# State space branch of a hybrid decoder block: constants of the preparation made once for all blocks

## The chip, the cores and the metric

The kernel runs on one core of a Trainium2 chip. The metric is the device time of one execution in microseconds (us). Three executions of the kernel before took 3461.62, 3467.05 and 3470.55 us; the median, 3467.05 us, is the time that the prediction is made against.

## What is computed

A decoder block for 2048 tokens of width 1024: norm, one projection, a state space branch and a sparse attention branch side by side, gates, an output projection, and a SwiGLU network. The change touches the state space branch alone. For each of 32 groups (16 channels in, 64 complex states) the reference computes

```python
abar = exp(A * dt)                                   # complex, per group and state
b    = coef * einsum('gnp,blgp->blgn', B, u)         # complex
s_l  = abar * s_(l-1) + b_l                          # over the 2048 tokens
y    = einsum('gpn,blgn->blgp', C_re, s_r) - einsum('gpn,blgn->blgp', C_im, s_i) + D * u
```

and then a gelu and a gated linear layer.

## The kernel before

**The branch by chunks.** The kernel cuts the 2048 tokens into 256 chunks of 8 (TC = 8, NCH = 256). Two groups lie on the 128 partitions (2 x 64 states) and are called a pair here: there are 16 pairs (NS), worked off in 8 blocks of two (NBLK = 8, SB = 2). For each block `ssm` (line 1340) needs some matrices that depend on the parameters only: G = C times the powers 0 to 8 of abar, E = B times the powers 7 to 0, transposed to ET, M, which carries the outputs within a chunk (it is filled by DMAs from K0, the product of B and G, with D on its diagonal), and pc, the 256 phases by which the chunks' states are turned so that a real scan can run over them.

**Two streams.** `prepare` (line 1353) makes these matrices for one block after another, mostly on POOL: complex products by `cmul` (line 1232), six operations each, a seventh to negate. G and E are made pair by pair (lines 1363 to 1374). Bk, the padded B, is cleared and filled per block (1377 to 1382), K0 is a product on PE copied out by ACT (1383 to 1392), D is added (1394 to 1397), M is cleared (1398, 1399) and filled by 16 DMAs (1402 to 1406), ET comes from PE and ACT (1407 to 1414), and pc from eight doublings, rows of 1, 2, 4 ... 128 phases for two pairs (1416 to 1426). A block is begun when the block two before it is solved (1355).

`solve` (line 1435) takes a block's inputs U, transposes them (Ut), multiplies by ET, turns by pc, scans on DVE, turns back into S (1480 to 1492; POOL clears its first column, 1483 and 1484), has POOL clear F and ACT copy Gr and Gi into it (1495 to 1502), multiplies S by F and Ut by M on PE, and copies the sum out as Y (1503 to 1517). `gelu` (1521) ends the block while the next is solved. All three use one PSUM bank ("sp"), one step after another; F lies in the buffer of `ee`.

**What sets the order.** Each engine works off its own queue in order. A planner (`Pace`, from line 52) lays these queues out when the kernel is built: streams are generators that yield what they wait for, and `Pace` takes the first stream whose need is met at PE's planned time, in the order state space branch, attention, dense part (`run`). Every instruction is booked at an estimated cost; on POOL that is 2.25 ns an element and 0.07 us:

```python
    RATE = {"DVE": (1.05e-3, 0.07), "ACT": (0.84e-3, 0.06), "POOL": (2.25e-3, 0.07)}   # line 58
            cost = size * r + c
```

The profile shows the helper's line, 206, for all of them, so the rows are told apart by their tiles. Beside the state space branch run the first four tiles of attention (scores, top-k search on DVE and ACT, softmax) and, filling PE, the gate matmuls of the dense part: tiles gps of 24 matmuls in two PSUM banks, evicted by ACT to gsg, with weights gw split into two parts by whichever of POOL, DVE and ACT the planner thinks free (`Loader.split`). After the state space branch comes its gated layer (`glu`, line 1557), and only then (`gated`) the rest of attention and the dense blocks, whose matmuls are called f.

Of the kernel before, what the change touches and what calls it, by code (L numbers as in the profile page):

```python
# [12 lines left out]
F32 = mybir.dt.float32  # L13
# [4 lines left out]
AF = mybir.ActivationFunctionType  # L18
ALU = mybir.AluOpType
# [16 lines left out]
G = 32  # L36
NST = 64
PG = 16
SW = G * PG
TC = 8  # L40
# [11 lines left out]
class Pace:  # L52
# [95 lines left out]
    def at(self, eng, *what):  # L148

        return lambda: self.when(eng, what) + (None,)  # L150
# [215 lines left out]
class Block:  # L366
# [851 lines left out]
            tt(s, s, q, op=ALU.mult)  # L1218
        return s, v

    def cmul(self, e, outr, outi, ar, ai, br, bi, t1, t2, neg_i=False):

        e.tensor_tensor(t1, ar, br, op=ALU.mult)
        e.tensor_tensor(t2, ai, bi, op=ALU.mult)
        e.tensor_tensor(outr, t1, t2, op=ALU.subtract)
        e.tensor_tensor(t1, ar, bi, op=ALU.mult)
        e.tensor_tensor(t2, ai, br, op=ALU.mult)
        e.tensor_tensor(outi, t1, t2, op=ALU.add)
        if neg_i:
            e.tensor_tensor(outi, self.zeros[:, :1].to_broadcast(list(outi.shape)), outi, op=ALU.subtract)  # L1230

    def ssm_params(self, pr, wk, ps_t, queue):

        nc, a = self.nc, self.a
        NS = G // 2
# [22 lines left out]
        for n in ("C_re", "C_im"):  # L1258
            t = pr.tile([128, NS, PG], F32, name=n)
            ap = a[n]  # L1260
            for b in range(2):
                raw = wk.tile([128, 2, NST], F32, name=f"{n}{b}")
                for sp in range(8):
                    o = ap.offset + (b * 16 + sp * 2) * PG * NST
                    sync.dma_start(raw[sp * PG:(sp + 1) * PG],
                                      bass.AP(tensor=ap.tensor, offset=o, ap=[[NST, PG], [PG * NST, 2], [1, NST]]))

                def turn(raw=raw, t=t, b=b):
                    ps = ps_t.tile([128, 512], F32, name="tp")
                    nc.tensor.transpose(ps[:, :128], raw.rearrange("p a n -> p (a n)"), self.ident)  # L1270
                    nc.scalar.copy(t[:, b * 8:(b + 1) * 8].rearrange("p s c -> p (s c)"), ps[:, :128])
                turns.append(turn)
            C.append(t)
        ar, ai = A["A_re"], A["A_im"]
# [65 lines left out]
    def ssm(self, st, params):  # L1340
# [8 lines left out]
        NEVER = ("PE", 1e9, None)  # L1349
        made = deque()  # L1350
        taken = [0]

        def prepare():
            for blk in range(NBLK):
                yield lambda: self.pace.idle("POOL") if blk < taken[0] + 2 else NEVER
                s0 = blk * SB
                ss = slice(s0, s0 + SB)

                Gr, Gi = (wk.tile([128, SB, TC + 1, PG], F32, name=f"G{n}", bufs=2) for n in "ri")
                Er, Ei = (wk.tile([128, SB, TC, PG], F32, name=f"E{n}") for n in "ri")  # L1360
                t1 = wk.tile([128, SB, TC + 1, PG], F32, name="t1")
                t2 = wk.tile([128, SB, TC + 1, PG], F32, name="t2")
                for sp in range(SB):
                    q = s0 + sp
                    shp = [128, TC + 1, PG]
                    pa = [z[:, q, :, None].to_broadcast(shp) for z in (ap_r, ap_i)]
                    cc = [z[:, q, None, :].to_broadcast(shp) for z in C]
                    yield self.pace.idle("POOL", ap_i)
                    cmul(gp, Gr[:, sp], Gi[:, sp], cc[0], cc[1], pa[0], pa[1], t1[:, sp], t2[:, sp], neg_i=True)
                    shp = [128, TC, PG]  # L1370
                    pa = [z[:, q, TC - 1::-1, None].to_broadcast(shp) for z in (ap_r, ap_i)]
                    bb = [z[:, q, None, :].to_broadcast(shp) for z in Bb]
                    yield self.pace.idle("POOL")
                    cmul(gp, Er[:, sp], Ei[:, sp], bb[0], bb[1], pa[0], pa[1], t1[:, sp, :TC], t2[:, sp, :TC])

                yield self.pace.idle("POOL")
                Bk = wk.tile([128, 2, SB, 2, PG], F32, name="Bk")
                gp.memset(Bk, 0.0)
                for i in range(2):
                    for g2 in range(2):  # L1380
                        pl = slice(g2 * 64, (g2 + 1) * 64)
                        gp.tensor_copy(Bk[pl, i, :, g2], Bb[i][pl, ss])
                yield at("PE", Bk, Gr, Gi, psp.free_at("sp"))
                ps = psp.tile([128, 512], F32, name="sp")
                for sp in range(SB):
                    o = ps[:32, sp * 128:(sp + 1) * 128]
                    nc.tensor.matmul(o, Bk[:, 0, sp].rearrange("p a c -> p (a c)"),
                                     Gr[:, sp, :TC].rearrange("p t c -> p (t c)"), start=True, stop=False)
                    nc.tensor.matmul(o, Bk[:, 1, sp].rearrange("p a c -> p (a c)"),
                                     Gi[:, sp, :TC].rearrange("p t c -> p (t c)"), start=False, stop=True)  # L1390
                K0 = wk.tile([32, SB, TC, PG], F32, name="K0")
                nc.scalar.copy(K0.rearrange("p s t c -> p (s t c)"), ps[:32, :SB * 128])
                yield self.pace.idle("POOL", K0)
                dd = wk.tile([32, SB, PG], F32, name="dd")
                gp.tensor_tensor(dd, eye[:, None, :].to_broadcast([32, SB, PG]),
                                 Ds[:, ss, None].to_broadcast([32, SB, PG]), op=ALU.mult)
                gp.tensor_tensor(K0[:, :, 0], K0[:, :, 0], dd, op=ALU.add)
                M = wk.tile([128, GB, 128], F32, name="M", bufs=2)
                gp.memset(M, 0.0)
                Mv = M.rearrange("p (s a) c -> p s a c", a=2)  # L1400
                yield at("SP", K0, M)
                for ta in range(TC):
                    for g2 in range(2):
                        nc.sync.dma_start(Mv[ta * PG:(ta + 1) * PG, :, g2, ta * PG:],
                                          K0[g2 * PG:(g2 + 1) * PG].rearrange("p s t c -> p s (t c)")
                                          [:, :, :128 - ta * PG])
                ET = wk.tile([128, 2, SB, 128], F32, name="ET", bufs=2)
                for i, E in enumerate((Er, Ei)):
                    yield at("PE", E, psp.free_at("sp"), wk.free_at("ET", 2) if i == 0 else 0.0)
                    ps = psp.tile([128, 512], F32, name="sp")  # L1410
                    for sp in range(SB):
                        nc.tensor.transpose(ps[:, sp * 128:(sp + 1) * 128],
                                            E[:, sp].rearrange("p t c -> p (t c)"), self.ident)
                    nc.scalar.copy(ET[:, i].rearrange("p s n -> p (s n)"), ps[:, :SB * 128])

                pc = [wk.tile([128, SB, NCH], F32, name=f"pc{n}", bufs=2) for n in "ri"]
                t1, t2 = (wk.tile([128, SB, NCH // 2], F32, name=f"pt{n}", tag=f"t{n}") for n in "12")
                yield self.pace.idle("POOL", wt[1])
                gp.memset(pc[0][:, :, 0:1], 1.0)
                gp.memset(pc[1][:, :, 0:1], 0.0)  # L1420
                for j in range(NW):
                    n = 1 << j
                    wr, wi = (z[:, ss, j:j + 1].to_broadcast([128, SB, n]) for z in wt)
                    cmul(gp, pc[0][:, :, n:2 * n], pc[1][:, :, n:2 * n], pc[0][:, :, :n], pc[1][:, :, :n], wr, wi,
                         t1[:, :, :n], t2[:, :, :n])
                    yield self.pace.idle("POOL")
                made.append((Gr, Gi, M, ET, pc))

        def load(blk):
            U = wk.tile([128, 2, GB, 128], F32, name="U")  # L1430
# [4 lines left out]
        def solve(blk):  # L1435
            s0 = blk * SB
            U = Us.popleft()
            yield lambda: at("PE") if made else NEVER
            Gr, Gi, M, ET, pc = made.popleft()
# [51 lines left out]
            dv.tensor_tensor(x2, sc[1][:, :, c1], pc[0][:, :, c1], op=ALU.mult)  # L1491
            dv.tensor_tensor(Si[:, :, 1:], x1, x2, op=ALU.add)
            yield at("DVE")

            yield at("POOL", wk.free_at("ee"))
            F2 = wk.tile([128, 2, SB, 2, 128], F32, name="F2", tag="ee")
            gp.memset(F2, 0.0)
            yield at("ACT", F2)
            for i, z in enumerate((Gr, Gi)):
                for g2 in range(2):  # L1500
                    pl = slice(g2 * 64, (g2 + 1) * 64)
                    nc.scalar.copy(F2[pl, i, :, g2], z[pl, :, 1:].rearrange("p s t c -> p s (t c)"))
# [483 lines left out]
```

## Time and profile before

| | |
|---|---|
| three executions | 3461.62, 3467.05, 3470.55 us |
| the profiled execution | 3462.75 us |
| its span | 3460.6 us |
| busy: PE, DVE, ACT, POOL | 3201.6, 2133.6, 1261.8, 706.1 us |
| preparation of the eight blocks (first G to last phase) | about 366 to 746 us |
| state space branch, last output written | about 823 us |

The page gives shares of the whole span; the stages have different limits, so the rows below are cut to windows, given in microseconds from the span's start. "PE sp L206 <- ACT F L206: 19.0, 4, 6.3" reads: PE, about to write the tile sp, waited for ACT's writing of F, 19.0 us in total, 4 times, at most 6.3. In a timeline the bracket at a line's end is the idle time before it and what ended it. PEclk is the share of TensorE's full clock that was granted.

### The profile page before, as it was taken

Reading aid. Unit: us, or ns where it says so; the run is one execution under the profiler, and the core shown is the slowest. Engines: PE = TensorE matmul, PEld = TensorE weight load, DVE = VectorE, ACT = ScalarE, POOL = GpSimd, SP = SyncE. Lnnn points to the kernel's source line nnn. Section 1 sums busy time; section 2 is a strip of 40 time slices with the busy share of each in tenths; the row PEclk is TensorE's granted clock in tenths of the full one; section 3 lists DMA queues with packets and bytes.
Section 4 is the critical chain, followed back from the end, with each engine's and each line's share of the span. In section 5 each row is a group of like instructions: output and inputs, shape, how many; then the busy total and the mean of one; then the engine's idle time right before and its main releaser. Section 6 shows DMA issues by size and latency. Waiting matters only on the chain. (4 is left out here: it accounts for less than half of the span.)

```text
span 3460.6 us, 44348 instructions
## 1 busy us (share of the span) xinstructions
PE 3201.6 (93%) x16292; PEld 2698.5 (78%) x16292; DVE 2133.6 (62%) x4306; ACT 1261.8 (36%) x2187; POOL 706.1 (20%) x1003
## 2 busy tenths in 40 slices
PE   6999999898878999989889999988899999999999
PEld 5889777676756888767688888767788888798887
DVE  4565665656496666788776766996856664222222
ACT  3141444445542544465024444771233442010000
POOL 3333686852213122244100000001000000000000
PEclk8999999999988999999999999999999999999999
DMA  4834333433448566567755233556453324755544
GB/s 134 248 119 121 117 110 89 147 124 105 146 148 300 208 212 228 182 232 244 286 184 194 97 133 135 194 195 242 176 200 121 134 86 152 282 214 215 195 170 182
DMA packets 321529, 605.69 MB, mean 175 GB/s; under 512 B 52896, under 2 KB 205216, under 8 KB 290592
## 3 DMA queue, kind: packets, MB, share of 16 engines
q1 hardware_dynamic: 321312, 602.86, 49.9%
q8 instruction: 128, 2.10, 0.3%
q14 instruction: 89, 0.73, 0.1%
HBM read 434.71 MB, written 166.89 MB: 174 GB/s over the span
## 5 line engine op out<-in xcount | busy, mean ns | idle before, releaser
L206 PE MATMUL f<-h,ww 128*128 128x512 f32 (+1 forms) x4416 | 1012.8, 383 | 3.0 <-DVE h L206 1.4
L206 PEld LDWEIGHTS f<-h,ww 128*128 128x128 f32 x4416 | 800.6, 190 | 159.9 <-DVE h L206 2.2
L206 PE MATMUL f<-wd,at 128*128 128x512 f32 x2112 | 530.8, 403 | 60.4 <-ACT at L206 31.9
L206 PEld LDWEIGHTS f<-wd,at 128*128 128x128 f32 x2112 | 403.5, 194 | 156.3 <-ACT at L206 27.9
L206 PE MATMUL gps<-hT,gw 128*128 128x512 f32 x1536 | 390.5, 404 | 17.3 <-ACT gsg L206 14.7
L206 ACT ACTIVATE jka<-S,tr 128x1024 bf16<-128x1024 f32 (+6 forms) x217 | 305.6, 1408 | 172.4 <-DVE tr L206 127.0
L206 PEld LDWEIGHTS gps<-hT,gw 128*128 128x128 f32 x1536 | 287.9, 192 | 81.5 <-ACT gsg L206 17.3
L206 DVE TENSOR_TENSOR x<-f,x 128x512 f32<-128x512 f32 x352 | 237.2, 686 | 91.3 <-PE f L206 90.5
L206 PE MATMUL mm<-w,hT 128*128 128x512 f32 (+1 forms) x1152 | 282.2, 403 | 7.4 <-DVE hT L206 7.1
L206 DVE SCALAR_TENSOR_TENSOR t<-t,f 128x512 f32<-128x512 f32 (+1 forms) x124 | 82.3, 664 | 329.5 <-PE f L206 284.4
L206 PEld LDWEIGHTS mm<-w,hT 128*128 128x128 f32 x1152 | 242.3, 241 | 32.5 <-DVE hT L206 8.5
L206 DVE TENSOR_TENSOR tl<-pt,th 128x512 fp32r<-128x512 f32 (+1 forms) x288 | 183.9, 658 | 131.7 <-ACT th L206 130.4
L206 ACT CAST th<-pt 128x512 fp32r<-128x512 f32 (+1 forms) x288 | 156.0, 563 | 233.5 <-PE pt L206 231.5
L206 POOL TENSOR_TENSOR g<-g,g 128x512 f32<-128x512 f32 x32 | 42.1, 1317 | 915.9 <-issue 551.8
L206 PE MATMUL f<-act,ww 128*128 128x512 f32 x768 | 190.8, 410 | 29.2 <-DMA act<-act 9.0
L206 PE MATMUL f<-ww,mg 128*128 128x256 f32 x1536 | 197.6, 291 | 18.3 <-DMA ww<-wc 10.0
L206 PEld LDWEIGHTS f<-ww,mg 128*128 128x128 f32 x1536 | 193.8, 199 | 21.3 <-issue 8.5
L206 PEld LDWEIGHTS f<-act,ww 128*128 128x128 f32 x768 | 150.8, 199 | 69.0 <-issue 14.3
L206 ACT ACTIVATE P<-P,m 128x1024 f32<-128x1024 f32 (+7 forms) x192 | 172.1, 899 | 72.6 <-DVE m L206 72.0
L206 PE MATMUL lg<-kk,q 128*128 128x512 f32 (+1 forms) x640 | 184.1, 390 | 5.8 <-DMA kk<-kk 3.7
L206 ACT ACTIVATE t<-f 128x512 f32<-128x512 f32 (+1 forms) x92 | 53.0, 576 | 331.7 <-PE f L206 331.6
L206 ACT CAST at<-t 128x512 fp32r<-128x512 f32 (+1 forms) x92 | 55.2, 600 | 325.2 <-DVE t L206 325.1
(347 smaller groups left out, 4577.1 us busy)
## 6 DMA issues: line engine op xcount, KB each, us to landing
ww<-wc SPq DMA_DIRECT2D x180, 1024.0 KB, 5.0
wd<-wc SPq DMA_DIRECT2D x66, 1024.0 KB, 8.5
wc<-ww SPq DMA_DIRECT2D x60, 1024.0 KB, 7.8
raw<-in_w_in_dram SPq DMA_DIRECT2D x104, 256.0 KB, 3.3
wc<-wd SPq DMA_DIRECT2D x22, 1024.0 KB, 7.5
x<-in_x_dram SPq DMA_DIRECT2D x32, 512.0 KB, 5.2
gate<-gsg SPq DMA_DIRECT2D x64, 256.0 KB, 2.2
g<-gate SPq DMA_DIRECT2D x64, 256.0 KB, 5.3
```

The lines of the kernel that those rows point to most:

```text
L206: return f(*args, **kw)
```

## The change

All in the state space branch:

- G and E are made for both pairs of a block in one complex product. The minus of G's imaginary part is taken into C_im when it is transposed (ACT scales by -1), so the negation goes.
- Bk (padded B, now for all 16 pairs, filled by four copies on ACT), dd (D on its diagonal) and the zeros of M and F are made once, ahead of the first block. M and F have two fixed buffers each, taken in turn, whose zeros stay.
- The first 32 phases of all 16 pairs are made once, into p0, in block 0; each block copies its 32 and doubles three times, to 64, 128 and 256.
- F is filled in `prepare`, by the same four copies on ACT per block, right after E has been issued and ahead of K0; the clearing in `solve` is gone. G has one buffer instead of two, and F one of its own.

```diff
-    def cmul(self, e, outr, outi, ar, ai, br, bi, t1, t2, neg_i=False):
+    def cmul(self, e, outr, outi, ar, ai, br, bi, t1, t2):
...
-                    nc.scalar.copy(t[:, b * 8:(b + 1) * 8].rearrange("p s c -> p (s c)"), ps[:, :128])
+                    nc.scalar.activation(t[:, b * 8:(b + 1) * 8].rearrange("p s c -> p (s c)"), ps[:, :128], AF.Copy,
+                                         scale=sign)
...
         def prepare():
+            yield self.pace.idle("POOL")
+            Bk = wk.tile([128, 2, NS, 2, PG], F32, name="Bk")
+            gp.memset(Bk, 0.0)
+            for i in range(2):
+                for g2 in range(2):
+                    pl = slice(g2 * 64, (g2 + 1) * 64)
+                    nc.scalar.copy(Bk[pl, i, :, g2], Bb[i][pl])
+            dd = wk.tile([32, NS, PG], F32, name="dd")
+            gp.tensor_tensor(dd, eye[:, None, :].to_broadcast([32, NS, PG]), Ds[:, :, None].to_broadcast([32, NS, PG]),
+                             op=ALU.mult)
+            Ms = [wk.tile([128, GB, 128], F32, name=f"M{i}") for i in range(2)]
+            Fs = [wk.tile([128, 2, SB, 2, 128], F32, name=f"F{i}") for i in range(2)]
+            for z in Ms + Fs:
+                gp.memset(z, 0.0)
+            p0 = [wk.tile([128, NS, N0], F32, name=f"p0{n}") for n in "ri"]
...
-                    cmul(gp, Gr[:, sp], Gi[:, sp], cc[0], cc[1], pa[0], pa[1], t1[:, sp], t2[:, sp], neg_i=True)
...
-                    cmul(gp, Er[:, sp], Ei[:, sp], bb[0], bb[1], pa[0], pa[1], t1[:, sp, :TC], t2[:, sp, :TC])
...
+                tt(t1, cr, pr, op=ALU.mult)
+                tt(t2, ci, pi, op=ALU.mult)
+                tt(Gr, t1, t2, op=ALU.add)
+                tt(t1, ci, pr, op=ALU.mult)
+                tt(t2, cr, pi, op=ALU.mult)
+                tt(Gi, t1, t2, op=ALU.subtract)
...
+                cmul(gp, Er, Ei, bb[0], bb[1], pa[0], pa[1], t1[:, :, :TC], t2[:, :, :TC])
+                F2 = Fs[blk % 2]
+                yield at("ACT", Gi)
+                for i, z in enumerate((Gr, Gi)):
                     for g2 in range(2):
                         pl = slice(g2 * 64, (g2 + 1) * 64)
-                        gp.tensor_copy(Bk[pl, i, :, g2], Bb[i][pl, ss])
+                        nc.scalar.copy(F2[pl, i, :, g2], z[pl, :, 1:].rearrange("p s t c -> p s (t c)"))
...
-                M = wk.tile([128, GB, 128], F32, name="M", bufs=2)
-                gp.memset(M, 0.0)
+                M = Ms[blk % 2]
...
-                for j in range(NW):
+                for j in range(N0.bit_length() - 1 if blk else 0, NW):
                     n = 1 << j
...
+                    if n == N0:
+                        for z in range(2):
+                            gp.tensor_copy(pc[z][:, :, :N0], p0[z][:, ss])
...
-            yield at("POOL", wk.free_at("ee"))
-            F2 = wk.tile([128, 2, SB, 2, 128], F32, name="F2", tag="ee")
-            gp.memset(F2, 0.0)
-            yield at("ACT", F2)
-            for i, z in enumerate((Gr, Gi)):
-                for g2 in range(2):
-                    pl = slice(g2 * 64, (g2 + 1) * 64)
-                    nc.scalar.copy(F2[pl, i, :, g2], z[pl, :, 1:].rearrange("p s t c -> p s (t c)"))
```

## Rows read from the trace of the kernel before

**Rows 1.** The page, busy time of the engines over the span.
```profile
PE 3201.6 (93%) x16292; PEld 2698.5 (78%) x16292; DVE 2133.6 (62%) x4306; ACT 1261.8 (36%) x2187; POOL 706.1 (20%) x1003
```
**Rows 2.** Busy time by window: length, PE, PEld, DVE, ACT, POOL, PEclk, DMA share, GB/s.
```profile
366.00:746.00 380.00, 342.72 (x1700) 271.39 (x1700) 230.24 (x549) 174.78 (x389) 294.35 (x712) 0.94 0.38 116
...
1011.00:3460.00 2449.00, 2307.51 (x11886) 1951.29 (x11884) 1523.22 (x2834) 830.64 (x1306) 232.54 (x135) 0.97 0.53 194
```
**Rows 3.** Waits of PE, 366 to 825 us: total, times, longest.
```profile
PE sp L206 <- ACT F L206: 19.0, 4, 6.3
PE sp L206 <- POOL pcr L206: 5.8, 1, 5.8
PE sp L206 <- POOL Bk L206: 5.2, 4, 2.8
...
PE sp L206 <- ACT Y L206: 1.8, 2, 1.0
```
**Rows 4.** Timeline, 402 to 496 us: start, duration, engine, operation, tiles, count.
```profile
402.44 3.02 PE L206 MATMUL gps<-hT,gw 128*128 128x512 f32 x12
...
485.91 0.73 DVE L206 TENSOR_TENSOR S<-sct,ee 128x510 f32<-128x510 f32 x1
...
491.78 0.95 POOL L206 MEMSET F<- 128x1024 f32 x1
...
492.77 0.82 ACT L206 COPY F<-Gr 64x256 f32<-64x256 f32 x2 [7.32 <-POOL F L206]
...
493.73 2.05 PE L206 MATMUL sp<-F,S 128*128 128x256 f32 x4 [5.79 <-POOL pcr L206]
```
**Rows 5.** Timeline of PE alone, two other waits.
```profile
421.49 0.64 PE L206 MATMUL sp<-Gr,Bk 128*32 128x128 f32 x2 [2.82 <-POOL Bk L206]
...
733.36 2.05 PE L206 MATMUL sp<-F,S 128*128 128x256 f32 x4 [4.19 <-ACT F L206]
```
**Rows 6.** Busy time by window again; the clock is the third number from the right.
```profile
420.00:745.00 325.00, 292.05 (x1468) 232.22 (x1468) 196.15 (x425) 147.61 (x329) 249.39 (x599) 0.93 0.38 116
490.00:500.00 10.00, 6.27 (x15) 4.95 (x16) 5.73 (x14) 2.69 (x7) 9.06 (x21) 0.66 0.34 94
```
**Rows 7.** Groups of POOL's instructions by form, 366 to 746 us: count, busy us, mean ns.
```profile
L206 POOL TENSOR_TENSOR gw<-raw,gw 128x512 fp32r<-128x512 f32 x13 | 19.8, 1521 | 21.5 <-ACT gw L206 21.3
...
L206 POOL COPY Bk<-Bb 64x32 f32<-64x32 f32 x32 | 9.8, 306 | 1.6
L206 POOL TENSOR_TENSOR t<-C_im,pwi 128x144 f32<-128x144 f32 x16 | 9.0, 560 | 0.0
...
L206 POOL TENSOR_TENSOR Gi<-zeros,Gi 128x144 f32<-128x144 f32 x16 | 6.8, 428 | 1.3
L206 POOL MEMSET F<- 128x1024 f32 x7 | 6.7, 953 | 0.0
L206 POOL TENSOR_TENSOR pcr<-pt,pt 128x256 f32<-128x256 f32 x8 | 6.3, 790 | 0.6
...
L206 POOL TENSOR_TENSOR pcr<-pt,pt 128x128 f32<-128x128 f32 x8 | 3.7, 458 | 0.6
...
L206 POOL TENSOR_TENSOR pcr<-pt,pt 128x2 f32<-128x2 f32 x8 | 3.5, 434 | 0.6
...
L206 POOL TENSOR_TENSOR pcr<-pt,pt 128x64 f32<-128x64 f32 x8 | 2.6, 320 | 0.6
L206 POOL TENSOR_TENSOR pcr<-pt,pt 128x32 f32<-128x32 f32 x8 | 2.1, 260 | 0.6
```
**Rows 8.** ACT, 366 to 825 us: its wait for F, and the copies of Gr into F.
```profile
ACT F L206 <- POOL F L206: 36.0, 6, 10.7
...
L206 ACT COPY F<-Gr 64x256 f32<-64x256 f32 x16 | 6.4, 403 | 36.1 <-POOL F L206 36.0
```
**Rows 9.** Timeline of PE, 836 to 838 us, at the start of the gated layer.
```profile
837.19 1.22 PE L206 MATMUL gps<-hT,gw 128*128 128x512 f32 x2 [9.29 <-ACT gsg L206]
```
**Rows 10.** Timeline of PE, 1671 to 1673 us, in a dense block.
```profile
1671.48 2.08 PE L206 MATMUL f<-wd,at 128*128 128x512 f32 x4 [15.52 <-ACT at L206]
```

More of the change, by code (lines that the diff above doesn't have):

```diff
@@ L1228, in cmul @@
         e.tensor_tensor(outi, t1, t2, op=ALU.add)
-        if neg_i:
-            e.tensor_tensor(outi, self.zeros[:, :1].to_broadcast(list(outi.shape)), outi, op=ALU.subtract)
     def ssm_params(self, pr, wk, ps_t, queue):
@@ L1266, in ssm_params, with turn @@
                                       bass.AP(tensor=ap.tensor, offset=o, ap=[[NST, PG], [PG * NST, 2], [1, NST]]))
-                def turn(raw=raw, t=t, b=b):
+                def turn(raw=raw, t=t, b=b, sign=-1.0 if n == "C_im" else 1.0):
                     ps = ps_t.tile([128, 512], F32, name="tp")
                     nc.tensor.transpose(ps[:, :128], raw.rearrange("p a n -> p (a n)"), self.ident)
-                    nc.scalar.copy(t[:, b * 8:(b + 1) * 8].rearrange("p s c -> p (s c)"), ps[:, :128])
+                    nc.scalar.activation(t[:, b * 8:(b + 1) * 8].rearrange("p s c -> p (s c)"), ps[:, :128], AF.Copy,
+                                         scale=sign)
                 turns.append(turn)
@@ L1351, in ssm @@
         taken = [0]
+        NS, N0 = G // 2, 32
         def prepare():
+            yield self.pace.idle("POOL")
[13 more added lines that the diff above has]
+            p0 = [wk.tile([128, NS, N0], F32, name=f"p0{n}") for n in "ri"]
             for blk in range(NBLK):
@@ L1357, in prepare @@
                 ss = slice(s0, s0 + SB)
-                Gr, Gi = (wk.tile([128, SB, TC + 1, PG], F32, name=f"G{n}", bufs=2) for n in "ri")
+                Gr, Gi = (wk.tile([128, SB, TC + 1, PG], F32, name=f"G{n}") for n in "ri")
                 Er, Ei = (wk.tile([128, SB, TC, PG], F32, name=f"E{n}") for n in "ri")
@@ L1362, in prepare @@
                 t2 = wk.tile([128, SB, TC + 1, PG], F32, name="t2")
[L1363 to L1368, printed above, removed]
-                    cmul(gp, Gr[:, sp], Gi[:, sp], cc[0], cc[1], pa[0], pa[1], t1[:, sp], t2[:, sp], neg_i=True)
[L1370 to L1373, printed above, removed]
-                    cmul(gp, Er[:, sp], Ei[:, sp], bb[0], bb[1], pa[0], pa[1], t1[:, sp, :TC], t2[:, sp, :TC])
+                shp = [128, SB, TC + 1, PG]
@@ new lines, in prepare @@
+                pr, pi = (z[:, ss, :, None].to_broadcast(shp) for z in (ap_r, ap_i))
+                cr, ci = (z[:, ss, None, :].to_broadcast(shp) for z in C)
+                yield self.pace.idle("POOL", ap_i)
+                tt = gp.tensor_tensor
+                tt(t1, cr, pr, op=ALU.mult)
[4 more added lines that the diff above has]
+                tt(Gi, t1, t2, op=ALU.subtract)
@@ L1376, in prepare @@
+                shp = [128, SB, TC, PG]
+                pa = [z[:, ss, TC - 1::-1, None].to_broadcast(shp) for z in (ap_r, ap_i)]
+                bb = [z[:, ss, None, :].to_broadcast(shp) for z in Bb]
                 yield self.pace.idle("POOL")
-                Bk = wk.tile([128, 2, SB, 2, PG], F32, name="Bk")
-                gp.memset(Bk, 0.0)
-                for i in range(2):
+                cmul(gp, Er, Ei, bb[0], bb[1], pa[0], pa[1], t1[:, :, :TC], t2[:, :, :TC])
+                F2 = Fs[blk % 2]
@@ L1386, in prepare @@
                     o = ps[:32, sp * 128:(sp + 1) * 128]
-                    nc.tensor.matmul(o, Bk[:, 0, sp].rearrange("p a c -> p (a c)"),
+                    nc.tensor.matmul(o, Bk[:, 0, s0 + sp].rearrange("p a c -> p (a c)"),
                                      Gr[:, sp, :TC].rearrange("p t c -> p (t c)"), start=True, stop=False)
-                    nc.tensor.matmul(o, Bk[:, 1, sp].rearrange("p a c -> p (a c)"),
+                    nc.tensor.matmul(o, Bk[:, 1, s0 + sp].rearrange("p a c -> p (a c)"),
                                      Gi[:, sp, :TC].rearrange("p t c -> p (t c)"), start=False, stop=True)
@@ L1393, in prepare @@
                 yield self.pace.idle("POOL", K0)
[L1394 to L1397, printed above, removed]
-                M = wk.tile([128, GB, 128], F32, name="M", bufs=2)
-                gp.memset(M, 0.0)
+                gp.tensor_tensor(K0[:, :, 0], K0[:, :, 0], dd[:, ss], op=ALU.add)
+                M = Ms[blk % 2]
                 Mv = M.rearrange("p (s a) c -> p s a c", a=2)
@@ L1418, in prepare @@
                 yield self.pace.idle("POOL", wt[1])
-                gp.memset(pc[0][:, :, 0:1], 1.0)
-                gp.memset(pc[1][:, :, 0:1], 0.0)
-                for j in range(NW):
-                    n = 1 << j
-                    wr, wi = (z[:, ss, j:j + 1].to_broadcast([128, SB, n]) for z in wt)
-                    cmul(gp, pc[0][:, :, n:2 * n], pc[1][:, :, n:2 * n], pc[0][:, :, :n], pc[1][:, :, :n], wr, wi,
-                         t1[:, :, :n], t2[:, :, :n])
+                if blk == 0:
+                    u1, u2 = (t.rearrange("p s c -> p (s c)").rearrange("p (s c) -> p s c", s=NS) for t in (t1, t2))
+                    gp.memset(p0[0][:, :, 0:1], 1.0)
+                    gp.memset(p0[1][:, :, 0:1], 0.0)
+                for j in range(N0.bit_length() - 1 if blk else 0, NW):
+                    n = 1 << j
+                    if n < N0:
+                        q, sl, (x1, x2) = p0, slice(0, NS), (u1, u2)
+                    else:
+                        q, sl, (x1, x2) = pc, ss, (t1, t2)
+                    if n == N0:
+                        for z in range(2):
+                            gp.tensor_copy(pc[z][:, :, :N0], p0[z][:, ss])
+                    wr, wi = (z[:, sl, j:j + 1].to_broadcast([128, x1.shape[1], n]) for z in wt)
+                    cmul(gp, q[0][:, :, n:2 * n], q[1][:, :, n:2 * n], q[0][:, :, :n], q[1][:, :, :n], wr, wi,
+                         x1[:, :, :n], x2[:, :, :n])
                     yield self.pace.idle("POOL")
-                made.append((Gr, Gi, M, ET, pc))
+                made.append((F2, M, ET, pc))
         def load(blk):
@@ L1438, in solve @@
             yield lambda: at("PE") if made else NEVER
-            Gr, Gi, M, ET, pc = made.popleft()
+            F2, M, ET, pc = made.popleft()
             Ut = wk.tile([128, GB, 2, 128], F32, name="Ut")
```

## The prediction

> **What bounds the kernel now.** I read the page first: TensorE is busy for 93% of the span and POOL for 20% [rows 1]. Nothing that POOL does would count by that line alone, so I cut the span into stages. In the stage in which the state space blocks are prepared (366 to 746 us) POOL is busy for 294.35 of 380 us, 77%, and PE for 342.72; after 1011 us POOL is nearly idle and PE is busy for 2307.51 of 2449 us [rows 2]. So there are two questions: does POOL make PE stand in the first stage, and does PE's order then carry what is won to the end?
>
> The waits of PE answer the first. Between 366 and 825 us it stood 19.0 us for the copies of F on ACT, 5.8 us for what the profile calls pcr, and 5.2 us for Bk, in nine waits together, 30.0 us [rows 3]. ACT's own list says that it stood 36.0 us for POOL's F, in six waits, the longest 10.7 us [rows 8]. One of them in order of time: the state S is complete at 486.6 us (485.91 + 0.73), but POOL's clearing of F sits behind the chain of phases of a later block and starts only at 491.78; ACT copies at 492.77; PE's product with F and S starts at 493.73 after 5.79 us of nothing [rows 4]. The "pcr" of the second wait is that clearing too, by its neighbour in POOL's queue. There are five of this kind, the first this one, the last, of 4.19 us, ended at 733.36; the one for Bk at 421.49 is of the other kind [rows 5]. PE works its queue in order, so the gate matmuls that would fill the hole stand behind the product.
>
> The holes cost twice. In the ten microseconds in which the hole of 5.79 us lies the granted clock is 0.66, a mixture of the levels 2.4 and 1.2 GHz (a share of the time at the lower level takes half that share off the mean, and half that share off the work); over 420 to 745 us, where all but the first of the holes are, it is 0.93 with PE busy for 292.05 of 325 us [rows 6]. So PE stood for 33 us and lost some 0.07 x 292.05 = 20.4 us more to the lower level. I charge POOL with its part, 30.0/33 of it, 18.6 us. **At stake: 30.0 + 18.6 = 48.6 us.**
>
> Why POOL is late: the planner books a POOL operation at 2.25 ns an element plus 0.07 us (RATE, line 58). Six operations on a row of 2 elements are booked at 0.07 us each and take 0.434 [rows 7]; so in the plan POOL has time and in the trace it has a backlog, and whatever the solving stream puts in its queue comes late.
>
> **The change, part by part.** POOL's time per block, by the rows of the preparing stage [rows 7]:
> - G and E in one go for two pairs. Before: 12 operations of 144 elements at 0.560 = 6.7, two negations at 0.428 = 0.9, 12 of 128 at some 0.50 (the 0.560 scaled) = 6.0; together 13.6 us. After: 6 of 288 and 6 of 256. A wide one is in the rows as 0.790 us for 256; the step from 0.458 (128) to 0.790 (256) is 2.6 ns an element, so 0.87 for 288. 6 x 0.87 + 6 x 0.79 = 9.9. Saved 3.7. If a wide operation in three dimensions of its own went at the rate of two narrow ones nothing but the negations is saved (0.9); if at the price of one narrow one, 7.2.
> - Phases of rows shorter than 32: five widths of six operations, between 0.434 (2 elements) and 0.260 (32), at 0.347: 10.4 us. Two copies of 64 elements (0.320 each) come instead: 9.8 saved.
> - Bk's four copies at 0.306 = 1.2; F's clearing 0.95; M's, half as large, 0.5; dd some 0.3. Saved 2.95.
>
> That is 16.4 us a block, 131 us for eight. Once, ahead of block 0, come the clearing of Bk and two F (3 x 0.95), two M (1.0), dd (0.8) and the phases for 16 pairs, widths 16 to 256: 6 x (0.22 + 0.260 + 0.320 + 0.458 + 0.790) = 12.3 (the 0.22 for 16 elements is an estimate, below the row for 32): 17 us. POOL's net: 114 us less, about 180 of 294 us. The 17 us lie beside gate matmuls, which need no more than a few splits from POOL; without that cover they would delay the first block by 17 less 9.8 us and no other.
>
> **F moves from the solving to the preparing stream.** Its two engine parts move: the clearing is gone, and 32 copies of 0.403 us on ACT [rows 8] come up tens of microseconds before the product that reads them. They now stand ahead of the block's copies of K0 and ET on ACT and wait for POOL's Gi; queued behind them on ACT are the evictions of the gate matmuls, which PE waits for when both banks are full. No DMA moves: the 16 copies of K0 into M per block stay on SP in the same place, and so do the two clearings of S on POOL, which still go through its queue. The four ACT copies for Bk add 4 x 0.4 = 1.6 us once. C_im's sign costs nothing: a copy becomes a scaled copy of the same size. F no longer shares the buffer ee, so two waits fall away. G has one buffer instead of two: POOL must wait for the last readers of the block before, PE's products for K0 and ACT's copies, which by the order are done a whole block earlier. I cost that at nothing; the cover is POOL's E, phases and wait for the next block (some 15 us), without which it would cost one product and one copy, under 2 us a block.
>
> **What is late next.** With F there, the product waits for S, which was complete 7 us before [rows 4], or for the bank that ACT's copy of Y frees (there is one bank for all of a block's steps). The nearest row is PE's wait for Y, 1.8 us in two, 0.9 us each [rows 3]. Bounds per block: nothing, if gate matmuls stand between all steps, and 2.7 us, if it waits so three times. I take 1.25, nearer one wait than three, as most steps have gate matmuls between them: 10 us for eight blocks (0 to 22).
>
> **Sum.** 48.6 - 10 = 38.6 us. The profiled execution took 3462.75 us (span 3460.6), so 3424 us; the median of the three runs lies 4.3 us above that execution, so against it 3467.05 - 38.6 = **about 3429 us**. Does it reach the end? All that follows is queued on PE behind this stage: the gates' remainder, the gated branch, the dense blocks; after 1011 us PE stands only 141 us in 2449 [rows 2]. But the planner lays out all that follows anew, and there are single holes that come from its misplacing an instruction, such as 15.52 us behind a cast at 1671 us [rows 10]. One more or less of them is the spread I put on the carry, 16 us each way.
>
> **Rivals.**
> *Nothing comes of it.* POOL's stage is only the filler of a stage in which PE has enough other work: the same gate matmuls must run, and the holes come back elsewhere, at the hand-over to the gated branch, where PE stands 9.29 us for ACT [rows 9], or in the dense blocks. For it: PE is busy for 90% of the stage. Against: the holes are PE's own and named, and in order. The Trainium skill, page "Perfetto Trace Analysis", section "Identifying the Most-Contended Engine", speaks for this rival: it tells one to take the engine with the highest occupancy, and POOL's 20% of the span would be left alone; by it the sum would be nought. The rows of the stage, with 77%, decide against it. 3467 us.
>
> *ACT becomes the one that holds PE.* If POOL stays behind the plan, the copies of F, now early in ACT's queue, hold the gate evictions behind them. The place is ACT's queue in the preparing stream. Such a hold is in the trace: the 9.29 us for gsg [rows 9]. It decides from 48.6/8 = 6.1 us a block, holes and clock together. With holds of POOL's longest lateness, 10.7 us [rows 8], of which one free bank of gate matmuls hides a part (24 of them, at 3.02 us for 12 [rows 4] some 6 us), PE stands 4.7 us and loses some 3.4 to the clock (0.34 of ten microseconds [rows 6]): 8 x 8.1 = 65 us, less 48.6: 16 us slower, 3483 us. Against it: Gi is now made first and POOL has half its time free.
>
> *The change does half of it.* The planner gives splits of gate weights to whichever engine it thinks free; with POOL freer on paper it gives POOL more, at 1.52 us each [rows 7]. As many again as now (13) take 20 of the 114 us back, and if wide operations save only the negations, 8 x 2.8 = 22 more. POOL is then busy for two thirds of the stage and late half as often: 3467 - 20 = 3447 us.
>
> **How the numbers follow.** Forecast 0.60 (its own range 3402 to 3456: 48.6 us and 16 more won at one end, 38.6 less 12 and 16 at the other), half of it 0.10, nothing 0.17, ACT 0.13. Faster by over 0.3% (10 us, about what a measurement of this kernel can tell from no change): 0.70; within: 0.17; slower: 0.13. The range goes from 3402 to 3476, which takes in the case of no change and leaves out the slower case and the luckiest tail.
>
> **What would show it.** In the changed profile: POOL busy for some 180 us before its last phase, and no short row of phases after block 0; no wait of PE or ACT for POOL's F or Bk; the clock of the stage near 0.98; the gated branch beginning some 35 to 40 us earlier. The prediction is wrong if PE's holes stay under other names (ACT F waiting for Gi, gsg), or if the stage ends earlier and the last dense block does not.

## The result, and the profile after

The changed kernel took 3425.83 us, the median of four executions (3422.88 to 3427.56), beside 3467.89 for the kernel before: a ratio of 0.988, 95% interval 0.9863 to 0.9898. The profiled execution has a span of 3424.1 us, 36.5 less. In the later sets, beside which the experiments stand, the kernel before took 3461.10 to 3462.65 us and the change was not measured again: its gain is 42 us by its own set, some 36 by the later ones, and 36.5 between the two profiled executions, which are what is split up below. The forecast was 3429, the range 3402 to 3476.

The page after answers to [rows 1]: POOL's busy time fell by 67.5 us in 372 instructions fewer, PE's by 21.9 at the same number of matmuls.

```profile
PE 3179.7 (93%) x16292; PEld 2684.6 (78%) x16292; DVE 2150.5 (63%) x4299; ACT 1262.8 (37%) x2192; POOL 638.6 (19%) x631
```

The last gate matmul (gps) that is not part of the dense blocks ends at 1011.4 us before and at 975.7 after; I cut there. Busy time by window, columns as in [rows 2], first of before, then of after:

```profile
366.00:1012.00 646.00, 574.66 (x2868) 460.67 (x2868) 407.72 (x987) 324.28 (x657) 351.39 (x762) 0.95 0.37 113
1012.00:3460.00 2448.00, 2307.14 (x11884) 1951.29 (x11884) 1522.25 (x2831) 830.05 (x1306) 232.54 (x135) 0.97 0.53 194
```

```profile
366.00:708.00 342.00, 315.25 (x1618) 250.03 (x1619) 237.29 (x535) 171.06 (x386) 223.00 (x339) 0.98 0.39 121
366.00:976.00 610.00, 560.47 (x2876) 452.61 (x2876) 420.02 (x983) 327.27 (x666) 281.06 (x389) 0.98 0.39 120
976.00:3424.00 2448.00, 2299.51 (x11884) 1945.97 (x11884) 1528.37 (x2832) 829.12 (x1304) 236.10 (x136) 0.97 0.53 194
```

What follows the cut takes 2448 us in both: nothing was given back, nothing won. Ahead of it 36 us went: PE's idle time fell from 646 - 574.66 = 71.3 to 610 - 560.47 = 49.5 (21.8 us), and its busy time, for the same matmuls, by 14.2, at a granted clock of 0.98 instead of 0.95. The last phase is made at 709 us instead of 742; in the window of the preparation POOL is busy for 223.00 of 342 us instead of 294.35 of 380 [rows 2].

The waits of PE between 360 and 960 us (total, times, longest). In [rows 3] F, pcr and Bk stood here with 30.0 us; none of them is left. The first line lies behind the branch, from 770 us on; before, gsg had 10.4 us in this window, 9.29 of them in one wait [rows 9]. On the branch's own bank, sp, the front places are now those of S, z (2.8 us before) and Ut (0.2 before).

```profile
PE gps L206 <- ACT gsg L206: 9.4, 7, 2.5
PE sp L206 <- DVE S L206: 8.2, 4, 4.7
PE u L206 <- ACT t L206: 6.8, 8, 1.8
PE sp L206 <- DVE z L206: 6.1, 3, 4.3
PE sp L206 <- ACT Ut L206: 4.2, 4, 1.5
PE u L206 <- DVE yp L206: 3.1, 5, 1.0
PE sp L206 <- ACT Y L206: 2.3, 2, 1.3
```

The longest in PE's timeline: the product that waited 5.79 us for a clearing before [rows 4] now waits for the state itself.

```profile
656.17 1.19 PE L206 MATMUL sp<-F,S 128*128 128x256 f32 x2 [4.72 <-DVE S L206]
658.64 1.19 PE L206 MATMUL sp<-F,S 128*128 128x256 f32 x2 [1.28 <-DVE S L206]
676.84 1.11 PE L206 MATMUL sp<-ident,z 128*128 128x128 f32 x4 [4.29 <-DVE z L206]
```

The single hole of 15.52 us in a dense block [rows 10] is there again, 38 us earlier:

```profile
1633.75 6.50 PE L206 MATMUL f<-wd,at 128*128 128x512 f32 x17 [15.54 <-ACT at L206]
```

### The profile page after: what moved, and what is told of

It is laid out like the page before. It is cut to its first block, busy times and chain, and to the rows that moved or that the text cites. A ratio compares the mean times of both kernels' runs of the same rounds, so it can differ in the third digit from the quotient of the medians.

```text
span 3424.1 us, 43974 instructions
## 1 busy us (share of the span) xinstructions
PE 3179.7 (93%) x16292; PEld 2684.6 (78%) x16292; DVE 2150.5 (63%) x4299; ACT 1262.8 (37%) x2192; POOL 638.6 (19%) x631
## 5 line engine op out<-in xcount | busy, mean ns | idle before, releaser
L206 PE MATMUL f<-wd,at 128*128 128x512 f32 x2112 | 529.5, 402 | 63.9 <-ACT at L206 34.9
L206 PE MATMUL gps<-hT,gw 128*128 128x512 f32 x1536 | 383.6, 400 | 11.2 <-ACT gsg L206 10.0
L206 PE MATMUL f<-ww,mg 128*128 128x256 f32 x1536 | 193.5, 288 | 17.5 <-DMA ww<-wc 6.7
```

The costliest lines, as they stand in the source:

```text
L206: return f(*args, **kw)
```

## The experiments

The theory to test: PE stood because POOL was later than the planner's book said, not because POOL had too much to do. The rivals: POOL's amount of work as such; the place of F's filling; and a gain that the dense part gives or takes by its new layout. Times are medians of four executions (six for e2), ratios are against the kernel before on the same chip. "The cut" is again the end of the last of those gate matmuls, in the profiled execution; a table behind the last experiment has it for all runs.

**e1: F early alone.** The kernel before with two fixed F, cleared once, filled in `prepare`; all other work of POOL as it was.

```diff
+            Fs = [wk.tile([128, 2, SB, 2, 128], F32, name=f"F{i}") for i in range(2)]
+            for z in Fs:
+                gp.memset(z, 0.0)
...
+                F2 = Fs[blk % 2]
+                yield at("ACT", Gi)
...
+                        nc.scalar.copy(F2[pl, i, :, g2], z[pl, :, 1:].rearrange("p s t c -> p s (t c)"))
...
-            gp.memset(F2, 0.0)
...
-                        nc.scalar.copy(F2[pl, i, :, g2], z[pl, :, 1:].rearrange("p s t c -> p s (t c)"))
```

> The kernel before with one part of the change: F has two fixed buffers, cleared once, and is filled in the preparing stream; all of POOL's other work stays. Theory (PE's holes come from F's clearing standing behind POOL's backlog): the holes for F, 25 of the 30 us, and their clock go, PE's waits for Bk stay; some 30 us faster than before, about 3435 us. First rival (POOL's amount of work has to fall, or the lateness only moves on): ACT now waits for POOL's Gi by as much as it waited for F, gate evictions stand behind it, and less than 10 us are won, 3458 us or more. Second rival (the gain is an accident of a new order): any time between, with PE's holes of the same sum under other names.

3496.34 us, ratio 1.0095 (1.0079 to 1.0111): slower by 34 us. PE's waits and then ACT's, 366 to 800 us, in this kernel:

```profile
PE sp L206 <- ACT yT L206: 24.1, 5, 9.0
PE sp L206 <- DVE z L206: 14.9, 1, 14.9
PE sp L206 <- POOL Bk L206: 10.7, 2, 10.0
...
ACT F L206 <- POOL Gr L206: 36.2, 6, 9.4
```

The second rival of the prediction, in full: ACT stands 36.2 us at the head of its queue for a G that POOL has not made. What is held behind it is not a gate eviction, as I had priced, but the gelu's steps z and copy yT, on which the one bank "sp" hangs. The cut stands at 1032 us: 21 us are lost ahead of it, some 10 behind. Of the three expectations the first rival's came.

**e2: POOL's work cut, F as before.** The changed kernel, but F cleared by POOL and filled by ACT in `solve`, G with two buffers again.

```diff
-                F2 = Fs[blk % 2]
-                yield at("ACT", Gi)
...
-                        nc.scalar.copy(F2[pl, i, :, g2], z[pl, :, 1:].rearrange("p s t c -> p s (t c)"))
...
+            yield at("POOL", wk.free_at("ee"))
+            F2 = wk.tile([128, 2, SB, 2, 128], F32, name="F2", tag="ee")
+            gp.memset(F2, 0.0)
...
+                        nc.scalar.copy(F2[pl, i, :, g2], z[pl, :, 1:].rearrange("p s t c -> p s (t c)"))
```

> The changed kernel with F as before: cleared by POOL and filled by ACT in the solving stream, in the buffer of ee; everything that takes work from POOL stays changed. Theory (backlog): with some 70 us less on POOL in the stage the clearing comes in time, so most of the 36 us of the span stay won, 3430 to 3442 us, and PE's wait for F falls from 25 us to under 8. First rival (only where F is filled counts): the holes for F stay above 15 us and the time is 3455 us or more.

3452.05 us, ratio 0.9973 (0.9961 to 0.9986). POOL is busy for 217.25 us to the last phase, as little as in the change, and yet ACT waits for its F as long as before [rows 8]:

```profile
PE sp L206 <- ACT F L206: 21.5, 7, 5.9
...
ACT F L206 <- POOL F L206: 39.0, 6, 9.7
```

A quarter less work on POOL is worth 10 us as long as one urgent clearing stands behind its phases. The time lies between the two that were expected; the wait is the rival's.

**e3: F's zeros alone.** The kernel before with two fixed F, cleared once; the ACT copies stay in `solve`.

```diff
+            for z in Fs:
+                gp.memset(z, 0.0)
...
-            gp.memset(F2, 0.0)
```

> The kernel before with F in two fixed buffers, cleared once, but still filled in the solving stream: only POOL's eight clearings leave its queue, 7.6 us of work. Theory (it is the place of the clearing in POOL's queue, not its 0.95 us): nearly all that filling F early gives, about 3437 us, ACT not waiting for POOL before F at all. First rival (amount of POOL's work): 7.6 of 294 us change nothing, 3460 us or more. Second rival (the copies must be early too): PE still stands some 2 us a block for the four copies on ACT, 16 us with their clock, so about 3450 us.

3440.88 us, ratio 0.9939 (0.9923 to 0.9955): 22 us won, between the theory and its second rival. PE no longer waits for F, but POOL's lateness has gone over to the next thing that is asked of it (PE's waits, then ACT's, 366 to 800 us):

```profile
PE sp L206 <- POOL Bk L206: 22.9, 6, 8.0
...
ACT K L206 <- POOL dd L206: 26.8, 3, 10.0
```

**e4: only the book.** The kernel before with no instruction changed: while the state space branch is laid out the planner books a POOL operation at 0.20 us more than its elements, instead of 0.07.

```diff
+                self.pace.RATE = {**Pace.RATE, "POOL": (2.25e-3, 0.20)}
                 yield from self.ssm(st, ready)
+            self.pace.RATE = Pace.RATE
```

> The kernel before with one number of the planner changed while the state space branch is laid out: a POOL operation is booked at 0.20 us plus 2.25 ns an element instead of 0.07 plus 2.25 ns. No instruction is added or removed. Theory (POOL is late because the plan books too little): the plan puts the product behind the time at which F is really there and fills the gap with gate matmuls; PE's waits for F, pcr and Bk fall from 30 us to under 10 and some 25 us are won, about 3442 us, though the branch itself ends later than at 823 us. First rival (POOL's work bounds the stage): the holes turn into a longer branch, the gate matmuls run out sooner, and nothing is won, 3460 us or more.

3431.29 us, ratio 0.9907 (0.9891 to 0.9924): 31 us, where the change won 36 to 42, with all of POOL's old work. The cut lies at 974, 37 us earlier than before and where the change has it; what follows took 8 us longer. The clock ahead of the cut is 0.97 (the windows are those of the change):

```profile
366.00:976.00 610.00, 563.65 (x2868) 457.17 (x2868) 394.71 (x958) 319.80 (x656) 339.58 (x751) 0.97 0.39 120
976.00:3431.00 2455.00, 2314.82 (x11884) 1958.59 (x11884) 1531.52 (x2857) 833.60 (x1312) 257.61 (x146) 0.97 0.53 194
```

POOL's own operations for the branch took 286 us here and 284 before. The book also moved splits of gate weights: 41 instead of 52 fell to POOL ahead of the cut, so its busy time there is 12 us smaller (339.58, 351.39 before). By e2, where 76 us less to the cut won 10, that is worth little; POOL's amount was not the cost. PE's waits for it, up to the branch's end, are 11.5 us in this trace (pt 4.8, F 3.7, Bk 3.0) instead of 30.0 [rows 3]. The branch itself ends later, as expected: its gated layer begins at 858 us instead of 840.

**e5: e1 with e4's book.** Both edits above.

> The kernel of e1 (F filled early, the rest of POOL's work as before) with the booking of e4 (POOL at 0.20 us plus 2.25 ns while the branch is laid out). Theory (e1 lost because ACT was sent to copy G before POOL had made it, not because an early copy is bad in itself): the plan now sends ACT there when Gi is made, ACT's wait for G falls from 36 us to under 10, and the time comes to that of e4 or a little below, 3425 to 3438 us. Rival (F's copies ahead of the gelu's steps on ACT cost the branch whatever the booking): 3465 us or more.

3407.24 us, ratio 0.985 (0.9836 to 0.9865). This is 24 us below e4, below the change itself with POOL's work uncut, and 18 below the range expected. ACT's wait for G is 9.5 us in five (Gr 5.4, Gi 4.1; in e1 36.2 and 9.7), so the early F that cost 34 us in e1 costs nothing once POOL is booked right. That it gains 24 is not shown. Of the 28 us between the profiled executions of e4 and e5 only 5 lie ahead of the cut (974 to 969), where F is at work; 23 lie behind it (2457 to 2434), in the layout of a dense part that the edit does not touch.

**e6: the short phases back.** The changed kernel, but all eight doublings made per block.

```diff
-                for j in range(N0.bit_length() - 1 if blk else 0, NW):
+                for j in range(NW):
...
-                        for z in range(2):
-                            gp.tensor_copy(pc[z][:, :, :N0], p0[z][:, ss])
```

> The changed kernel with one part undone: every block makes all its phases again, so POOL has some 80 us more in the stage, of the short operations that the plan books too low; F stays early. Theory (an early F bears only so much lateness of POOL): ACT waits for G again, some 15 to 30 us in the stage, and half or more of the gain is lost, 3445 to 3490 us. Rival (the early F and the fixed zeros carry the gain, the phases nothing): within 8 us of the changed kernel, 3418 to 3434 us.

3474.59 us, ratio 1.0042 (1.0025 to 1.0059): all of the gain is lost and more, 49 us over the change, as the theory had it. Of the 47 us between the two profiled executions 39 lie ahead of the cut. PE's waits, then ACT's; the gelu's steps z stand on ACT right behind the copies that wait for G:

```profile
PE sp L206 <- DVE z L206: 23.1, 3, 11.9
...
ACT F L206 <- POOL Gr L206: 25.7, 6, 7.8
```

**e7: the change with e4's book.**

> The changed kernel with the booking of e4. Theory (the change and the right booking remove the same holes): PE no longer waits for POOL in the changed kernel, so nothing is left to win, 3418 to 3434 us. Rival (they remove different holes and add up): 3405 us or less.

3421.71 us (3410.57 to 3426.11), ratio 0.9883 (0.9865 to 0.9901), the change's own 0.988. The cut is at 976 again: ahead of it the book won nothing, as expected, though there was an error left for it to mend. Over all of POOL's operations for the branch, measured less booked (by line 58, or by 0.20 us in e4 and e7; clearings at 0.9 ns an element) is 102 us before, 14 in e4, 58 in the change and 15 in e7. So the 43 us that e7 mends had cost nothing.

**e11: G and E pair by pair again.** The changed kernel with 24 operations of 144 and 128 elements a block in place of 12 wide ones.

```diff
-                tt(t1, cr, pr, op=ALU.mult)
...
+                for sp in range(SB):
+                    tt(t1[:, sp], cr, pr, op=ALU.mult)
...
```

> The change with G and E made pair by pair again (40 short POOL operations more per phase of two pairs in place of the merged ones, the same elements). If the number of short operations decides, part of the holes come back: ACT waits for Gi with the early F on it, 3430 to 3445. If the merged operations saved nothing that counts, 3424 to 3428 as the change.

3428.31 us, ratio 0.9903 (0.9878 to 0.9929), not to be told from the change; the cut is at 973. The edit adds 12 operations a block, not the 40 of the expectation. ACT does wait 9.8 us for G again (nothing in the change), but no time hangs on it: the merged products save POOL 15 us (654.0 less 638.6 on the pages) that cost nothing.

**e8, e12, e9, e10: the other error of the book.** Behind the cut of the change PE's longest waits were for a cast of ACT ("at", 34.9 us) and for DVE's x and h (26.5 us together), tiles of the dense part in the queue that also holds the counts of the top-k search; so I looked there for a second booking error. A count with an accumulator is booked at half of DVE's rate, 1792 x 1.05 ns / 2 + 0.07 + 0.14 = 1.15 us; DVE's groups by form, kernel before, behind the cut, show

```profile
L206 DVE TENSOR_SCALAR_CACHE_REDUCE jkd<-H,tf 128x1792 bf16<-128x1792 uint16 x16 | 33.2, 2076 | 0.4
```

The edit is one condition; e8 puts it into the change, e12 into the kernel before, e9 into e4, e10 into e5.

```diff
-            elif eng == "DVE" and op in ("tensor_scalar", "tensor_tensor") and short:
+            elif eng == "DVE" and op in ("tensor_scalar", "tensor_tensor") and short and "accum_out" not in kw:
```

> The changed kernel with another booking put right, as a look for a version that beats both: a count of the top-k search on DVE over 1152 two-byte elements takes 1.41 us and is booked at 0.81 (the planner halves it). Theory (DVE is late in the dense part as POOL was here): the hole of 15.5 us behind a cast in a dense block and a part of the waits for DVE's x, h and un go, 15 to 30 us faster than the changed kernel, about 3400 us. Rival (the search, laid out more slowly, ends later and the dense blocks run out of work): 3425 us or more.

> The kernel before with two bookings of the planner mended and no instruction changed: POOL at 0.20 us + 2.25 ns per element while the branch is laid out, and DVE's counts with accumulation at full cost. If the two errors are separate (one costs PE before the gates' end, the other behind it), the times add: 3431 less some 53 us, about 3378, the gates' end at 976 and the rest some 2395. If they share the same slack, about 3405 to 3420.

> As e5 (F cleared once and filled early, all of POOL's old work, POOL booked at 0.20 us + 2.25 ns per element) with DVE's counts at full cost as well. If the gains add: 3407 less some 53, about 3354, below every other version. If e5's lead over the change was an accident of one layout, it lands with e8, at 3370 to 3380.

> The kernel before with DVE's counts with accumulation booked at full cost and no instruction changed. If that error acts behind the gates' end alone and the change ahead of it alone, it takes from the kernel before what it takes from the change, 53 us: about 3410. If the gain hangs on the layout that it meets (with POOL booked right on the kernel before it took 26, on the early F 6), it is 5 to 30 us: 3433 to 3458.

e8 took **3373.15 us, ratio 0.9746 (0.9731 to 0.976)**, the best version of all; e12 3420.03 (0.9867; 0.9843 to 0.9891), e9 3405.07 (0.9844; 0.9822 to 0.9866), e10 3401.15 (0.9825; 0.9804 to 0.9847). Behind their own cuts, e8 and then e12 by window:

```profile
967.00:3366.00 2399.00, 2295.08 (x11884) 1945.03 (x11884) 1526.97 (x2852) 831.36 (x1312) 264.09 (x146) 0.98 0.54 198
```

```profile
1006.00:3421.00 2415.00, 2300.67 (x11884) 1946.62 (x11884) 1529.67 (x2839) 829.53 (x1307) 261.37 (x146) 0.98 0.54 197
```

Most of the gain lies behind the cut: by the profiled executions 48 of 57 us in e8 and 34 of 39 in e12. The rest lies ahead, 9 us (976 to 967) and 5 us (1011 to 1006). PE's wait for ACT behind the cut, before and in the change, then in e8:

```profile
PE f L206 <- ACT at L206: 31.9, 7, 15.5
```

```profile
PE f L206 <- ACT at L206: 34.9, 7, 15.5
```

```profile
PE f L206 <- ACT at L206: 11.5, 5, 5.7
```

The edit takes 53 us from the change (46 by the ratios, as the change stands beside a slower set), about twice what was expected of e8, and 41 from the kernel before, between the two figures expected of e12. Where POOL is booked right it takes less: 26 us upon e4 (the case of a shared slack) and 6 upon e5, where neither figure expected came true: e5's lead over the change is gone, and e10 does not come down to e8 either. In e9 and e10 DVE has 2923 and 2907 instructions behind the cut, in e12 2839, so part of the attention's search is laid out behind it there; why the planner does so was not followed further and stays open.

Medians in us of the study, the rows by what was done to POOL:

| | F late, as before | F early | F late, counts booked | F early, counts booked |
|---|---|---|---|---|
| POOL as before | 3462.6 | 3496.3 (e1) | 3420.0 (e12) | not tried |
| POOL's work cut | 3452.1 (e2) | 3425.8 (the change) | not tried | 3373.2 (e8) |
| POOL booked right | 3431.3 (e4) | 3407.2 (e5) | 3405.1 (e9) | 3401.2 (e10) |
| both | not tried | 3421.7 (e7) | not tried | not tried |

The profiled executions, split at the cut (us):

| | cut | behind it | | cut | behind it |
|---|---|---|---|---|---|
| before | 1011 | 2449 | e6 | 1015 | 2456 |
| the change | 976 | 2448 | e7 | 976 | 2432 |
| e1 | 1032 | 2460 | e11 | 973 | 2445 |
| e2 | 1000 | 2451 | e8 | 967 | 2400 |
| e3 | 987 | 2454 | e12 | 1006 | 2416 |
| e4 | 974 | 2457 | e9 | 968 | 2432 |
| e5 | 969 | 2434 | e10 | 970 | 2438 |

Without the edit to the counts the part behind the cut ranges over 28 us, though no edit is meant for it. The profiled execution of e7 was its fastest, 11 us under its median. What these edits do to POOL is therefore read ahead of the cut.

## Why the prediction held, point by point

**What is at stake, 48.6 us.** Right in kind: the nine waits for F, pcr and Bk are gone, and the clock with them rose. Up to the cut PE's idle time fell by 21.8 us, and the clock gave 14.2 of the 18.6 charged to POOL: 36.0 in sum, against 38.6 in the forecast. (Two of the nine waits, 1.7 us, end before 420 us, outside the window of the 33; the charge should have been 28.3/33, 17.5 us.)

**What is late next was mis-sized**, 10 us forecast, 19.1 measured. I had named S or the bank freed by Y and sized it by Y. Y stayed small, 2.3 us. But PE's waits on the bank sp fell only from 35.2 to 24.2 us up to the cut: in place of the 30.0 came S with 8.2, and more of Ut (4.0), of z (3.3) and of four others (3.6). That the idle time still fell by as much as forecast is luck: some 10 us more went in waits that the forecast did not name, 4.7 of them for gsg (14.7 to 10.0, behind the branch) and 3.6 for the loads qi and kk of the attention.

**POOL's saving was mis-sized**: 114 us forecast, 71 measured (294.35 to 223.00). Adding up POOL's groups by what they write up to the last phase: G, E and their terms 104 to 71 us, where I gave them 30 (the 0.560 that I took for the narrow operations was a slow group's, their mean is 0.50; the wide ones took 0.78 and 0.70 instead of 0.87 and 0.79); the cleared and padded tiles 26 to 4, as forecast; splits of gate weights 21 to 26; but the phases (pt, pcr, pci, p0) only 148 to 118, 30 saved instead of 66. The short rows and their 77 us did go, for 23 us of p0 and copies; but I had let the rows of 64 and more keep their duration, and they took 95 us instead of 71:

```profile
L206 POOL TENSOR_TENSOR pcr<-pt,pt 128x128 f32<-128x128 f32 x8 | 6.0, 745 | 0.6
...
L206 POOL TENSOR_TENSOR pt<-pcr,wtr 128x64 f32<-128x64 f32 x8 | 5.5, 685 | 0.0
...
L206 POOL COPY pcr<-p0r 128x64 f32<-128x64 f32 x8 | 5.2, 649 | 0.0
```

0.458 became 0.745 for 128 elements, and the copies that I priced at 0.320 took 0.649 [rows 7]. It did not hurt, since POOL's amount was not what PE waited for (e2, e4, e11).

**Why POOL is late** was the prediction's last step on the profile, and e4 shows it by itself. But the prediction then counted POOL's microseconds as if each were worth the same. They are not, by the pages' busy time of POOL (638.6 us in the change): 15 us more cost no time (e11), 54 more cost 49 (e6), 10 fewer came with 26 us more (e2), and the 80 more of e4 with 5. The first two differ by the book. The thirty short operations of a block are booked at 0.098 us on the mean of the five widths and took 0.32 (77 us for 240): 6.7 us a block that the plan did not know of. The 24 narrow products of G and E are booked at 0.394 and 0.358 and took about 0.51 and 0.505: 12 x 0.116 + 12 x 0.147 = 3.2, and the 12 wide ones are still 0.7 over. That the phases matter and the merge does not is shown; this reason for it is only worked out from rows, and it is not the whole reason. In sum over the branch (measured less booked) e11 is 78 us short and e6 90, the change 58, and e2, which still has 21.5 us of waits for F, only 50. So lateness costs past some slack that no run measured, and what slack there is depends on when the late thing is asked for.

**The carry.** 2448 us behind the cut in both. The 16 us that I had put on the new layout were about the size: without the edit to the counts, e1 to e7 and e11 have 2432 to 2460 there. That a better book takes 34 to 48 us out of that part was not in the prediction, and not of the change.

**Signs.** The short rows went after block 0, the clock of the stage is 0.98, no wait for POOL's F is left, and one of ACT for Bk, 2.8 us, came at the start. But the gated layer began 62 us earlier (its first matmul at 778 instead of 840 us), not 35 to 40: I had taken the branch's end for the measure of what is won. It is not. In e4 the gated layer begins 18 us later than before and the gate matmuls end 37 us earlier; in e6 it begins 31 us earlier and they end 4 us later. What counts is how long PE stands while the same matmuls run.

**Rivals.** ACT holding PE was real and worse than priced where POOL stays late (e1: 34 us slower, 21 of them ahead of the cut, forecast 16; e6: 13 us), with another victim, the bank "sp". The change avoids it only because the short phases went in the same edit. "Nothing comes of it" and "half of it" did not come.

## What to carry to other kernels

Where queues are laid out ahead by estimated costs, compare each engine's booked with its measured cost per operation, short ones above all: an engine at 20% of the span cost some 36 us by being later than the plan, and mending one constant gave most of that back without touching an instruction. Not every error of the book costs: the change leaves 58 of the 102 us, and mending 43 of those won nothing ahead of the cut. Issue work early on a shared queue only when its producer is on time; up to the point where the change stops acting, the same move cost 21 us with POOL late and gained 5 with POOL on time. Where every edit lays out anew all that follows, split the time at that point before a difference is put down to the edit. Try the parts of such a change apart: here two parts gained 10 and lost 34 us alone and gained 36 together, and one part was worth nothing.

## What the runs showed of the hardware

POOL's short operations take about as long as the operation of DVE beside them when that one reads two tiles from SBUF. In the change 47 of the 52 operations of 64 elements on phases ran for a third of their time or more beside a two-input operation of DVE and took 0.63 us on the mean; before, 32 of 48 found DVE idle for most of their time and took 0.30. In the change, POOL and DVE in order of time (start, duration), while the solving stream turns and scans:

```profile
607.24 0.74 DVE L206 TENSOR_TENSOR ee<-ee,pci 128x512 f32<-128x512 f32 x1
607.38 0.69 POOL L206 COPY pcr<-p0r 128x64 f32<-128x64 f32 x1
608.02 0.69 DVE L206 TENSOR_TENSOR ee<-ee 128x512 f32<-128x512 f32 x1
608.02 0.78 POOL L206 COPY pci<-p0i 128x64 f32<-128x64 f32 x1
608.75 0.69 DVE L206 TENSOR_TENSOR_SCAN ee<-m,sct 128x256 f32<-128x256 f32 x1
608.77 0.75 POOL L206 TENSOR_TENSOR pt<-pcr,wtr 128x64 f32<-128x64 f32 x1
609.35 0.72 DVE L206 TENSOR_TENSOR_SCAN sct<-m,ee 128x256 f32<-128x256 f32 x1
609.49 0.67 POOL L206 TENSOR_TENSOR pt<-pci,wti 128x64 f32<-128x64 f32 x1
```

In the kernel before, an operation of 32 elements beside such a one of DVE, and one of 64 with DVE idle:

```profile
489.41 0.69 DVE L206 TENSOR_TENSOR gw<-raw,gw 128x512 fp32r<-128x512 f32 x1
489.44 0.77 POOL L206 TENSOR_TENSOR pt<-pci,wti 128x32 f32<-128x32 f32 x1
...
492.94 0.30 POOL L206 TENSOR_TENSOR pt<-pci,wti 128x64 f32<-128x64 f32 x1
```

0.77 us for 32 elements, 0.30 for 64: the neighbour counts for more than the size, and a booked cost by elements cannot hold on POOL beside such operations. The Trainium skill, page "SBUF — State Buffer", section "SBUF: two separate sides", says that DVE and GpSimd share a pair of ports by an exclusive lock, held for a whole instruction, also where DVE reads two inputs from SBUF; these rows agree, while no run here isolates the port.
